# A two-layer decoder step: layer 0's second half by block products in twelve slices, layer 1's weight sums on VectorE

## The chip, the cores and the metric

The kernel runs on one core of a Trainium2 chip. The metric is the device time of one execution in microseconds; lower is better. TensorE (PE) multiplies matrices, VectorE (DVE) and ScalarE (ACT) do elementwise work, GpSimd (POOL) issues some DMAs, and SyncE (SP) issues the rest.

## The reference, cut to what matters

Two layers work on 1024 prompt tokens and on 8 sample tokens with the same weights. Each layer has a mixer and a SwiGLU FFN, with a norm before and after each:

```python
def swiglu(h, w_gu, w_down):
    gate, up = jnp.split(h @ w_gu, 2, axis=-1)
    return (jax.nn.silu(gate) * up) @ w_down
...
        hn = rmsnorm(h, g[0])
        if l < N_A:
            mix, S = a_mixer(...)      # gated linear recurrence, and attention into 256 memory tokens
        else:
            mix = b_mixer(...)         # stick-breaking attention, and attention into 256 memory tokens
        h = h + rmsnorm(mix, g[1])
        h = h + rmsnorm(swiglu(rmsnorm(h, g[2]), w_gu[l], w_down[l]), g[3])
```

The model width is 1024, the inner width of the FFN is 2816. All data is float32.

## The kernel before, in words

**Tokens and tiles.** Activations lie transposed, 128 features to a partition block, so a width of 1024 is a list of eight tiles. The tokens are two groups: group 0 has 512 prompt tokens, group 1 has 512 prompt and the 8 sample tokens (520, handled as two halves of 260). A number is kept as two parts, a rounded one (`fp32r`) and the rest: `split_to` makes both with a ScalarE cast (L227) and a VectorE subtraction (L228). Weights are loaded in blocks of 512x128 and split in the same way (`split_w`, L206 and L207; in `gate_up_w` L501 and L502). Each product is three matmuls: high by high, high by low, low by high.

**The FFN.** The inner width is 22 slices of 128, in five parts: `PARTS = [(0, 5), (5, 5), (10, 4), (14, 4), (18, 4)]`. For each part the slices' gate and up projections are made, then the part's share of the down projection is added to `R`. There are three ways to make a slice:

- `ffn.part` uses `proj` (L220), with two double PSUM banks, and `silu` by Exp, Ln and Exp.
- `gate_up_q` (L464) is the same product in four single banks, with the table's Silu. For a slice of group 1 both take 8 x 2 x 3 x 2 = 96 matmuls of 260 columns. While it runs it steps `sums_w`, the generator that makes the sums of the operands that the next form needs.
- `gate_up_w` (L511) sees gate and up, the two halves of the width and the two halves of the tokens as a 2x2 by 2x2 block product and takes seven products in place of eight: 7 x 4 x 3 = 84 matmuls. It needs four sums of weight blocks and, from `sums_w`, four sums of operand blocks.

`ffn_w` runs a part by the last two forms: its argument `steps` has one entry for each ordinary slice, with how many steps of `sums_w` to take in it, and its argument `first` is the part with which it starts.

**The weights' sums.** `weight_sums(l, parts)` makes the four sums in DRAM: 16 steps for each part of five or four slices, each step one GpSimd DMA, half of them with an addition in the DMA. Before each DMA a one-element copy on GpSimd (L563) ties it to the work of the moment. Layer 0 has them for the parts 2, 3 and 4, layer 1 for all five (80 steps, spread over the middle of the kernel). `gate_up_w` then loads seven blocks for a slice, four of them sums.

**The order of the work.** `weave` interleaves generators in given proportions, in program order. A list scheduler turns that order into a fixed queue for each engine, taking what is ready first by priority of program order; at run time a queue is in order. Around the change the order is: group 0's queries for layer 1 (`b0.heads`) with the end of group 1's output projection (`o1.finish`); group 0's two attentions (`b0.sb`, `b0.mem`), woven with the parts 0 and 1 of group 1's FFN of layer 0; that FFN's parts 2 to 4; group 0's output projection (`o0.mm`) with group 1's norm, its K/V projection and its queries; group 1's attention beside group 0's FFN of layer 1; and last group 1's FFN of layer 1 by `ffn_w(1, 1, ...)`, with three ordinary slices and nineteen by products.

**Buffers that matter.** Raw weight blocks have five tiles (`wraw`) and, in `ffn_w`, others by turns; split blocks five (`wspl`) and by turns some of four (`cpool`). The tag `x0` has eight tiles, which before hold the two attentions' split outputs of group 0 from the attention until `o0.mm`. The middle results of a part are tiles of `mpool`, which has five.

Of the kernel before, what the change touches and what calls it, by code (L numbers as in the profile page):

```python
# [18 lines left out]
P = 128  # L19
# [4 lines left out]
def tile_decoder(  # L24
# [204 lines left out]

    def silu(dst, ps, g):  # L230
# [48 lines left out]
    def sums_w(g, xs, ops, YT, ZT):  # L279
# [5 lines left out]
        for k in range(4):  # L285
# [15 lines left out]
            b11, b12, b21, b22 = full(x0, 0), full(x0, h), full(x1, 0), full(x1, h)  # L301
# [150 lines left out]
    def gate_up_q(g, l, f, xt, side, n_side, first):  # L452
# [4 lines left out]
        for j in range(2):  # L457
# [14 lines left out]
            for a in range(2):  # L472
                d = sg[:, a * h : (a + 1) * h]
                if j == 0:
                    act[0] = nc.scalar.activation(d, pp[a][:, :h], AF.Silu)
                else:
                    nc.vector.tensor_mul(d, d, pp[a][:, :h])
# [4 lines left out]
    def gate_up_w(g, l, f, ops, spl, raws):  # L482
# [5 lines left out]
        src = [  # L488
            (w_gu[l][0:512, gate : gate + P], 0), (sums[l][part][0][:, o : o + P], 4), (sums[l][part][1][:, o : o + P], 5),
            (w_gu[l][512:D, gate : gate + P], 1), (sums[l][part][2][:, o : o + P], 6), (sums[l][part][3][:, o : o + P], 2),  # L490
            (w_gu[l][512:D, up : up + P], 3),
        ]

        def weight(j):
            r = raws()
            nc.sync.dma_start(r, src[j][0].rearrange("(k p) m -> p k m", p=P))
            return r.rearrange("p k m -> p (k m)")

        def split(src):
# [3 lines left out]
            return w  # L503

        def product(ps, j, first=False):
            w = split(weight(j))
            i = src[j][1]
# [16 lines left out]
        nc.scalar.activation(sg[:, :h], pa[:, :h], AF.Silu)  # L524
        product(pb, 4)
        dt = T()
        nc.scalar.copy(dt[:, h:n], pd[:, :h])
        gt = T()
        nc.vector.tensor_add(gt[:, h:n], dt[:, h:n], pb[:, :h])
        product(pc, 5)  # L530
        nc.vector.tensor_sub(gt[:, :h], pc[:, :h], dt[:, h:n])
        product(pb, 6)
        act[0] = nc.scalar.activation(sg[:, h:n], gt[:, :h], AF.Silu)
# [41 lines left out]
    class ffn_w:  # L575


        def __init__(self, g, l, x, steps, first, rows, R=None, own=False):
# [3 lines left out]
            self.half = []  # L582

            def YT():
                if rows:
# [5 lines left out]
            self.sums = sums_w(g, x, self.ops, YT, YT if rows else lambda: A(F32R))  # L591

        def spl(self):
            self.n += 1
            if (self.pi or not self.rows) and not self.own and self.n % 8 in (1, 4, 6):
# [9 lines left out]
        def raws(self):  # L605
            self.r += 1
            if not self.rows and self.r % 2:
# [1029 lines left out]
```

## Time and profile before

| | |
|---|---|
| median of three runs | 2450.1 us (2447.81 to 2451.44) |
| profiled execution | 2446.43 us, span 2444.6 us |
| granted TensorE clock | 0.999 |
| TensorE busy | 2412.0 us |
| VectorE busy | 1639.0 us |
| ScalarE busy | 1251.2 us |
| GpSimd busy | 186.1 us |

The span is the time from the first to the last instruction of the program, and the busy times are unions over the engine's instructions. Matmuls overlap, so a matmul's mean duration is longer than the distance from one to the next. In the views below, a group's row ends with its busy time, the mean duration in ns, the idle time before its instructions and what ended that idle time; a row of windows gives for each engine the busy time in a stretch.

### The profile page before, as it was taken

The page shows a single profiled execution, that of the slowest core. Times are in us where ns is not written, and L with a number is a line of the kernel's source. Part 1 is how long each engine was busy: PE and PEld are TensorE (multiplying, and loading weights), DVE is VectorE, ACT ScalarE, POOL GpSimd, SP SyncE. Part 2 cuts the span into 40 slices and gives each one's busy share as a digit, 9 for nine tenths or more (in the row PEclk, how much of TensorE's full clock was granted, in tenths as well). Part 3 has the DMA queues.
Part 4 walks back from the last instruction along what each step waited for, and adds up shares of the span by engine and source line. Part 5 has one row for each costly group of instructions (what it writes and reads, how often), then busy time and mean ns, then how long its engine had stood idle before and what let it go on. Part 6 is the DMA issues. An engine that isn't in the chain of part 4 may idle for free.

```text
span 2444.6 us, 42106 instructions
## 1 busy us (share of the span) xinstructions
PE 2412.0 (99%) x15839; PEld 2159.3 (88%) x15839; DVE 1639.0 (67%) x2987; ACT 1251.2 (51%) x2441; POOL 186.1 (8%) x315
## 2 busy tenths in 40 slices
PE   8999999999999999999999999999999999999998
PEld 6888888888889988999999989877777888999998
DVE  5867557665897686654756686777788467755565
ACT  5547544344445555554434554555555445654445
POOL 1001101101000000111200102121000100000000
PEclk9999999999999999999999999999999999999999
DMA  5454666577746447677766649655354563464542
GB/s 187 120 166 117 161 191 158 134 192 186 209 132 172 123 156 232 179 179 168 196 166 165 202 139 293 196 151 150 99 163 121 145 192 119 140 193 144 148 145 73
DMA packets 534734, 397.42 MB, mean 163 GB/s; under 512 B 21325, under 2 KB 473018, under 8 KB 534530
## 3 DMA queue, kind: packets, MB, share of 16 engines
q1 hardware_dynamic: 505346, 315.02, 43.3%
q0 software_dynamic: 29184, 79.70, 14.1%
q8 instruction: 125, 2.05, 0.3%
q14 instruction: 79, 0.65, 0.1%
HBM read 364.81 MB, written 101.14 MB: 191 GB/s over the span
## 4 chain that ended last, share of the span: by engine, by line
PE 87%; DVE 6%; DMA 3%; issue 2%; ACT 2%; POOL 0%; SPq 0%; DVEq 0%; ACTq 0%; POOLq 0%
PE mm L220 46%; PE q L511 13%; PE q L648 9%; PE q L464 3%; PE mm L1042 2%; PE s L1188 1%; PE s L906 1%; PE s L1385 1%; PE mm L851 1%; PE mm L824 1%; PE s L875 1%; PE q L680 1%; PE s L1351 1%; DVE ws L207 1%; DMA b<-qd 1%
## 5 line engine op out<-in xcount | busy, mean ns | idle before, releaser
L220 PE MATMUL mm<-x,ws 128*128 128x260 f32 (+1 forms) x6240 | 1115.6, 335 | 3.5 <-DVE r L657 1.7
L220 PEld LDWEIGHTS mm<-x,ws 128*128 128x128 f32 x6240 | 941.0, 188 | 123.9 <-DVE x L228 2.1
L206 ACT CAST ws<-w 128x512 fp32r<-128x512 f32 (+1 forms) x652 | 382.3, 588 | 492.1 <-PE mm L220 336.2
L207 DVE TENSOR_TENSOR ws<-w,ws 128x512 fp32r<-128x512 f32 (+1 forms) x652 | 418.6, 648 | 246.0 <-ACT ws L206 232.0
L220 PE MATMUL mm<-m,ws 128*128 128x512 f32 (+1 forms) x1344 | 281.8, 361 | 0.5 <-DVE r L400 0.4
L220 PEld LDWEIGHTS mm<-m,ws 128*128 128x128 f32 x1344 | 217.8, 188 | 37.2 <-issue 1.0
L648 PE MATMUL q<-m,ws 128*128 128x260 f32 (+1 forms) x1824 | 222.0, 282 | 0.0
L648 PEld LDWEIGHTS q<-m,ws 128*128 128x128 f32 x1824 | 219.0, 188 | 1.3 <-DVE t L534 0.7
L502 DVE TENSOR_TENSOR ws<-w,ws 128x512 fp32r<-128x512 f32 x181 | 124.0, 690 | 89.7 <-ACT ws L501 86.3
L501 ACT CAST ws<-w 128x512 fp32r<-128x512 f32 x181 | 111.8, 621 | 110.8 <-PE q L648 31.9
L511 PE MATMUL q<-x,ws 128*128 128x260 f32 (+1 forms) x1188 | 158.1, 282 | 0.0
L511 PEld LDWEIGHTS q<-x,ws 128*128 128x128 f32 x1188 | 148.7, 188 | 0.0
L511 PE MATMUL q<-y,ws 128*128 128x260 f32 x912 | 119.7, 283 | 0.4 <-ACT q L521 0.4
L511 PEld LDWEIGHTS q<-y,ws 128*128 128x128 f32 x912 | 113.6, 188 | 0.9 <-ACT q L521 0.6
L464 PE MATMUL q<-x,ws 128*128 128x260 f32 (+1 forms) x720 | 91.3, 284 | 0.2 <-DVE r L400 0.2
L464 PEld LDWEIGHTS q<-x,ws 128*128 128x128 f32 x720 | 88.4, 188 | 1.8 <-DVE r L400 0.5
L511 PE MATMUL q<-a,ws 128*128 128x260 f32 (+1 forms) x672 | 87.0, 282 | 0.0
L511 PEld LDWEIGHTS q<-a,ws 128*128 128x128 f32 x672 | 83.2, 188 | 0.0
L657 DVE TENSOR_TENSOR r<-r,q 128x260 f32<-128x260 f32 (+1 forms) x128 | 48.4, 420 | 48.2 <-PE q L648 48.1
L237 DVE TENSOR_SCALAR t<-mm 128x512 f32<-128x512 f32 (+1 forms) x58 | 40.0, 690 | 48.6 <-PE mm L220 48.4
L563 POOL COPY mk<-a 128x1 f32<-128x1 f32 x36 | 21.9, 609 | 640.4 <-ACT a L1241 392.1
L566 POOL DMA_DIRECT2D wsum<-in_w_gu x64 | 58.5, 935 | 114.1 <-DMA wsum<-wsum 89.5
(355 smaller groups left out, 3027.8 us busy)
## 6 DMA issues: line engine op xcount, KB each, us to landing
w<-in_w_gu SPq DMA_DIRECT2D x297, 256.0 KB
w<-in_w_down SPq DMA_DIRECT2D x160, 256.0 KB
wsum<-in_w_gu POOLq DMA_DIRECT2D x72, 512.0 KB, 6.5
w<-wsum SPq DMA_DIRECT2D x104, 256.0 KB
w<-in_w_in_a SPq DMA_DIRECT2D x80, 256.0 KB
w<-in_w_o SPq DMA_DIRECT2D x64, 256.0 KB
wsum<-in_w_gu POOLq DMA_DIRECT2D x24, 640.0 KB, 6.8
wsum<-wsum POOLq DMA_DIRECT2D x24, 512.0 KB, 5.6
```

The source lines that it names most:

```text
L206: nc.scalar.copy(ws[:, 0, :n, :], raw[:, :n, :])
L207: nc.vector.tensor_sub(ws[:, 1, :n, :], raw[:, :n, :], ws[:, 0, :n, :].bitcast(F32))
L220: nc.tensor.matmul(ps[:, a, : PW[g]], wt, xt[k][:, xi, o : o + PW[g]], start=(k == 0 and wi == 0), stop=(k == nk - 1 and wi == 2),)
L237: nc.vector.tensor_scalar(sv(x, g), pv(ps, g), -44.0, None, op0=ALU.max)
L464: ins = nc.tensor.matmul(pp[a][:, :h], wt, xt[k][:, xi, a * h : (a + 1) * h], start=(k == 0 and wi == 0), stop=(k == ND - 1 and wi == 2),)
L501: nc.scalar.copy(w[:, 0, :], src)
L502: nc.vector.tensor_sub(w[:, 1, :], src, w[:, 0, :].bitcast(F32))
L511: nc.tensor.matmul(ps[:, :h], w[:, wj, k * P : (k + 1) * P], x[:, xi, :], start=(first and k == 0 and wi == 0), stop=(k == 3 and wi == 2), ...
L566: nc.gpsimd.dma_start(d, a, accum_op=ALU.add)
L648: nc.tensor.matmul(pp[a][:, :h], wt, mids[k][:, xi, a * h : (a + 1) * h], start=(k == 0 and wi == 0), stop=(k == nf - 1 and wi == 2),)
L657: nc.vector.tensor_add(d, d, pp[a][:, :h])
L1042: nc.tensor.matmul(pb[i][:, a, :], xt[k][:, xi, c * P : (c + 1) * P], ws[:, s, :], start=(k == 0 and wi == 0), stop=(k == ND - 1 and wi == 2),
```

## The change

The operands' sums for group 1's FFN of layer 0 are made beside group 0's attention, in the first three slices of part 0. The parts 0 and 1 are run by `gate_up_q` in place of `ffn.part`, in single banks, with Silu by Exp, Ln and Exp (`lean`) as `ffn.part` had it. The parts 2, 3 and 4 are then run by `gate_up_w` in all their twelve slices; before, three slices of part 2 were ordinary, with the sums made in them.

The sums take the eight tiles of `x0`. The attentions' outputs therefore go to DRAM as they are made (`put`) and come back by `load`, which reads them after part 2 and splits them beside part 4's down projection. The sums read the normalized rows from `o1.R` (`src`) and overwrite them; before, they added the two parts of each operand first.

The 80 steps of `weight_sums(1, ...)` are gone. In layer 1 `gate_up_w` loads the four raw blocks of a slice and makes the sums with four VectorE additions, one into a tile of `npool` and three in place. Where sums are in DRAM (layer 0), the slice is as before. The `lean` form of `gate_up_w` and the tiles in `spare` are for product slices beside an attention; with ten ordinary slices there are none here.

```diff
+    def put(xo, i, cols, src):
+        if isinstance(xo, list):
+            split_to((xo[i][:, 0, cols], xo[i][:, 1, cols]), src)
+            return
+        t = B()[:, : cols.stop - cols.start]
+        nc.scalar.copy(t, src)
+        nc.sync.dma_start(xo[:, i, cols], t)
...
-    def sums_w(g, xs, ops, YT, ZT):
+    def sums_w(g, xs, ops, YT, ZT, src=None):
...
-            b11, b12, b21, b22 = full(x0, 0), full(x0, h), full(x1, 0), full(x1, h)
+            if src:
+                b11, b12, b21, b22 = (src[i][:, c : c + h] for i in (k, k + 4) for c in (0, h))
+            else:
+                b11, b12, b21, b22 = full(x0, 0), full(x0, h), full(x1, 0), full(x1, h)
...
+    def gated(d, x):
+        nc.scalar.activation(d, x, AF.Exp, scale=-1.0)
+        nc.scalar.activation(d, d, AF.Ln, bias=1.0)
+        nc.scalar.activation(d, d, AF.Exp, scale=-1.0)
+        nc.vector.tensor_mul(d, d, x)
...
-                if j == 0:
+                if j == 0 and lean:
+                    if a == 0:
+                        x = T()
+                    nc.vector.tensor_scalar(x[:, a * h : (a + 1) * h], pp[a][:, :h], -44.0, None, op0=ALU.max)
+                    if a:
+                        gated(sg[:, :n], x[:, :n])
+                elif j == 0:
                     act[0] = nc.scalar.activation(d, pp[a][:, :h], AF.Silu)
...
+        ready = sums.get(l, {}).get(part)
...
+        raw = {}
+        if not ready:
+            raw = {"a11": load(block(0, gate)), "a21": load(block(0, up))}
+            raw.update(a22=load(block(512, up)), a12=load(block(512, gate)))
 
         def weight(j):
...
+            if j == 1:
+                s1 = N()[:, :512]
+                nc.vector.tensor_add(s1, raw["a21"], raw["a22"])
+                return s1
+            if j == 2:
+                nc.vector.tensor_add(raw["a21"], raw["a11"], raw["a21"])
+                nc.vector.tensor_add(raw["a11"], raw["a21"], raw["a22"])
+            if j == 5:
+                nc.vector.tensor_add(raw["a11"], raw["a11"], raw["a12"])
+            return raw[("a11", "", "a11", "a12", "a21", "a11", "a22")[j]]
...
+            if self.pi in self.beside and self.r % 9 < 4:
+                return self.spare[self.r % 9 // 2][:, self.r % 9 % 2].rearrange("p (k m) -> p k m", k=4)
+            if (not self.pi or not self.rows) and self.pi not in self.beside and self.r % 2:
                 return B().rearrange("p (k m) -> p k m", k=4)
-            if self.rows and self.pi and self.r % 2:
+            if self.rows and self.r % 2:
...
-            d = xo[H + h]
-            split_to((d[:, 0, :G], d[:, 1, :G]), po)
+            put(xo, H + h, slice(0, G), po)
...
-        def open(self):
-            self.xo = wo_tiles(self.g)
+        def open(self, dram=False):
+            self.xo = tc.dram_tile([P, ND, WID], F32, name=nm("xo")) if dram else wo_tiles(self.g)
+
+        def load(self):
+            d, n, self.xo = self.xo, NG[self.g], []
+            ts = []
+            for k in range(0, ND, 2):
+                t = A()
+                nc.sync.dma_start(t[:, :, :n], d[:, k : k + 2, :n])
+                ts += [t[:, 0, :n], t[:, 1, :n]]
+                yield
+            for t in ts:
+                x = X(self.g)
+                split_to((x[:, 0, :n], x[:, 1, :n]), t)
+                self.xo.append(x)
+                yield
...
-    ws = weight_sums(1, range(5))
...
-    weave((b0.heads(), 8), (o1.finish(), 17), (islice(ws, 4), 4))
-    b0.open()
+    weave((b0.heads(), 8), (o1.finish(), 17))
+    b0.open(True)
+    set_banks(True)
+    fw = ffn_w(1, 0, o1.x, (5, 6, 5, 0, 0, 0, 0, 0, 0, 0), 0, False, beside=(0, 1), src=o1.R)
+    weave((chain(b0.sb(), b0.mem()), 25), (chain(fw.part(0), fw.part(1)), 18))
+    p4 = fw.part(4)
+    back = b0.load()
+    drain(fw.part(2), islice(back, 4))
+    drain(fw.part(3), islice(p4, 4))
+    weave((p4, 4), (back, 8))
     f1 = ffn(1, 0, o1.x)
-    weave((chain(b0.sb(), b0.mem()), 25), (chain(f1.part(0), f1.part(1)), 18), (islice(ws, 34), 35))
-    set_banks(True)
-    fw = ffn_w(1, 0, o1.x, (5, 6, 5), 2, False, f1.R)
-    weave((chain(fw.part(2), fw.part(3), fw.part(4)), 24), (islice(ws, 8), 8))
-    f1.acc = fw.acc
+    f1.R, f1.acc = fw.R, fw.acc
     set_banks(False)
```

The other calls of `weave` lose their share of `ws` and are otherwise as before.

89 lines of the change are left out of this document (53 added, 36 removed).

## The prediction

> **What bounds the kernel now.** I read the page first: the busy shares, the chain that ended last and the DMA queues.
>
> ```profile
> span 2444.6 us, 42106 instructions
> PE 2412.0 (99%) x15839; PEld 2159.3 (88%) x15839; DVE 1639.0 (67%) x2987; ACT 1251.2 (51%) x2441; POOL 186.1 (8%) x315
> q0 software_dynamic: 29184, 79.70, 14.1%
> PE 87%; DVE 6%; DMA 3%; issue 2%; ACT 2%; POOL 0%; SPq 0%; DVEq 0%; ACTq 0%; POOLq 0%
> ```
>
> TensorE is busy for 99% of the span and carries 87% of the chain. So a matmul that is removed shortens the kernel by its own time, and work on other engines costs nothing until it makes TensorE wait. The question is therefore twofold: how many matmuls go, and where VectorE, which gets new work, comes near its own limit. The chain in order of time gives the price of a matmul where the change is made (start, length, what):
>
> ```profile
> 1184.33 24.96 PE mm L220 x209
> 1209.29 5.73 PE s L464 x48
> 1215.02 28.70 PE q L464 x240
> 1243.72 10.06 PE q L511 x84
> 1253.79 23.43 PE q L648 x192
> 1277.22 40.22 PE q L511 x336
> ```
>
> L464 is the ordinary slice (48 and 240 records make three slices of 96), L511 the slice by seven block products (84 each), L648 the down projection. There is no gap between the rows: this stretch runs at TensorE's pace, 40.22/336 = 0.1197 us a matmul, 10.06 us a product slice and 34.43/3 = 11.48 us an ordinary one.
>
> The windows show the other engines in the stretches that the change loads or relieves:
>
> ```profile
> core 0: us, PE busy (x) PEld busy (x) DVE busy (x) ACT busy (x) POOL busy (x), PEclk, DMA share, GB/s
> 990.00:1035.00 45.00, 45.00 (x356) 43.17 (x356) 26.51 (x46) 23.21 (x40) 6.45 (x12) 1.00 0.68 182
> 1026.00:1184.00 158.00, 157.35 (x1198) 148.22 (x1196) 88.00 (x166) 83.10 (x171) 22.78 (x48) 1.00 0.68 165
> 1184.00:1209.00 25.00, 25.00 (x210) 24.98 (x209) 24.78 (x63) 11.39 (x27) 7.86 (x9) 1.00 0.78 193
> 1380.80:1404.00 23.20, 23.20 (x193) 22.90 (x191) 16.05 (x30) 10.81 (x17) 2.16 (x4) 1.00 0.74 215
> 1460.00:1547.00 87.00, 86.28 (x690) 83.62 (x690) 59.17 (x102) 41.66 (x73) 23.17 (x33) 1.00 0.99 272
> 1547.00:1900.00 353.00, 346.00 (x1651) 267.67 (x1650) 272.21 (x424) 185.35 (x359) 26.81 (x26) 1.00 0.47 143
> 2280.70:2303.90 23.20, 23.20 (x195) 23.08 (x194) 13.61 (x28) 7.28 (x12) 0.00 (x0) 1.00 0.43 125
> 2303.90:2344.30 40.40, 40.40 (x338) 40.40 (x338) 25.55 (x46) 23.81 (x49) 0.00 (x0) 1.00 0.57 165
> ```
>
> The first two are the attention of the first token group beside the FFN of the second; 1184 to 1209 is the end of its part 1, where most of the operands' sums are made today; 1380 its last down projection; 1460 the K/V projection and heads, with the DMA engines full; 1547 the second attention; the last two a down projection and four product slices of layer 1. The row of 1184 matters most; the sums' lines run from its start to its end:
>
> ```profile
> 1184.42 0.42 DVE L298 TENSOR_TENSOR b<-x 128x260 f32<-128x260 f32 x1
> 1205.26 0.88 DVE L306 TENSOR_TENSOR b<-b,b 128x260 f32<-128x260 f32 x2
> ```
>
> VectorE is busy for 24.78 of 25 us there and TensorE loses nothing. A full VectorE alone is not yet a stall.
>
> **Part 1, three slices more by products.** Layer 0's second half has 13 ordinary slices and 9 product slices; after it, 10 and 12. Three times 96 - 84 = 12 matmuls go: 36 x 0.1197 = **-4.3 us**. All of them lie on the chain, so this counts in full. The down projections keep their count.
>
> **Part 2, the operands' sums beside the attention.** They need, from these groups:
>
> ```profile
> L306 DVE TENSOR_TENSOR b<-b,b 128x260 f32<-128x260 f32 (+1 forms) x48 | 20.0, 419 | 0.1
> L298 DVE TENSOR_TENSOR b<-x 128x260 f32<-128x260 f32 (+1 forms) x48 | 18.4, 419 | 0.0
> L228 DVE TENSOR_TENSOR m<-t,m 128x512 fp32r<-128x512 f32 (+1 forms) x88 | 60.8, 690 | 9.4 <-ACT m L227 8.7
> ```
>
> Each of the 16 steps is one subtraction and one split, 2 x 0.42 us of VectorE: 13.4 us. (L298, which re-adds the two halves of an operand, 16 x 0.42 us, goes: the sums read the normalized rows that still stand in out_proj's tiles.) The gate's clamp and the product come as two halves of 260 in place of one of 520, about 2 x 0.15 us a slice, 3 us over ten; the eight attention outputs lose their VectorE half of the split, 8 x 0.69 = 5.5 us. So VectorE gains some 11 us in a stretch where it now has 158 - 88 = 70 us free. They are concentrated, though: the 16 steps fall into the first three slices. By the row of 990 that stretch goes from 26.5 to some 41 busy us of 45, 91%. Four tiles that the middle results need are freed only as the steps finish, so a late step holds the next slice's evacuation. The bounds of this: nothing, by the row of 1184 (99% busy, no loss), and by the row of 1547, where VectorE is at 77% beside an attention and TensorE idles 7 of 353 us, 2% of the stage's some 190 us, 3.8 us. I take **+0.7 us**, nearer the first because the ten slices' matmuls do not read the sums at all.
>
> The Silu beside the attention is Exp, Ln, Exp as it is before, so ScalarE gets only 16 casts of 0.41 us. The four single banks replace two double ones, with the same two groups in flight: nothing.
>
> **Part 3, the attention's output through DRAM.** Eight copies and stores replace eight splits; four loads and eight splits come back beside the last down projection. The stores stand on SP's queue before later weight loads and wait for a ScalarE copy; with ten raw and split buffers ahead of TensorE (5 + 5, 24 matmuls or 2.9 us each) a wait of a few us is covered. The eight splits add 8 x 0.69 = 5.5 us to VectorE's 16.05 of 23.2: 21.6, it still fits. If they came late, out_proj would wait, and this seam is already bare:
>
> ```profile
> 1404.03 0.76 DVE L657 TENSOR_TENSOR r<-r,q 128x260 f32<-128x260 f32 x2 [0.73 <-PE q L648]
> 1404.93 5.79 PE L220 MATMUL mm<-x,ws 128*128 128x512 f32 x24 [0.90 <-DVE r L657]
> ```
>
> TensorE waits 0.90 us there for the last evacuation. Bounds: 0, and 5.5 us if all splits came after it. I take **+0.2 us**: the splits need tiles that the products free before that projection begins, so they can go early in it.
>
> **Part 4, layer 1's weight sums.** Eighty GpSimd DMA steps go, with their one-element copies. What this can give is TensorE's idle time in the stretches where they run: 0.65 us in 1026:1184 and 0.72 us in 1460:1547, where DMA is at 0.99. Bounds 0 and -1.4; I take **-0.7 us**. On POOL's own queue only the cache page loads of the second attention stand behind these steps; they can but come earlier. Against this VectorE gets four additions of 128x512 in each of 19 product slices. These are the rows for a slice:
>
> ```profile
> L502 DVE TENSOR_TENSOR ws<-w,ws 128x512 fp32r<-128x512 f32 x181 | 124.0, 690 | 89.7 <-ACT ws L501 86.3 <-DMA w<-wsum 1.0 <-DMA w<-in_w_down 1.0
> L501 ACT CAST ws<-w 128x512 fp32r<-128x512 f32 x181 | 111.8, 621 | 110.8 <-PE q L648 31.9 <-PE q L511 25.8 <-DMA w<-wsum 19.3
> L267 DVE TENSOR_TENSOR st<-st,n 128x512 f32<-128x512 f32 (+1 forms) x91 | 62.1, 690 | 2.1 <-ACT n L266 1.3
> L529 DVE TENSOR_TENSOR t<-t,q 128x260 f32<-128x260 f32 (+1 forms) x33 | 13.8, 419 | 10.8 <-PE q L511 9.5 <-ACT t L527 1.3
> 2234.52 1.29 DVE L502 TENSOR_TENSOR ws<-w,ws 128x512 fp32r<-128x512 f32 x2
> ```
>
> An addition costs 0.69 us (L267, the same form). Counted by durations a slice needs 7 x 0.69 (splits) + 4 x 0.69 (additions) + 4 x 0.42 + 0.69 = 9.96 us, against 10.06 of TensorE. But two in a row take 1.29, not 1.38: the second starts 0.60 after the first. The pair of 1404.03 does the same for 260 elements: 0.76 - 0.42 = 0.34. By starts it is 11 x 0.60 + 4 x 0.34 + 0.60 = 8.6 us, which leaves 1.5 us a slice for waits.
>
> Here a rule weighs against the change. The Trainium skill, "VectorE: DVE Perf Modes", section "The DRAIN you can't avoid", says that the next operation does not start until the pipe is empty, so that what counts is the number of operations. The row of 2234.52 shows an overlap of 0.09 us; by the rule a slice would be at 9.96 us and every wait would reach TensorE. The row decides here, and the third rival below is priced from the durations.
>
> What can wait: the cast of a summed operand (0.62 us, L501) lies between its addition and its split, three times a slice, some 2.4 us if the queue holds nothing in between. But the additions need only raw blocks that are loaded a slice ahead, so they can stand in today's idle time (40.40 - 25.55 us in four slices), as the sums do in the row of 1184. Over a whole part there is room: 25.55 + 13.61 + 11.0 = 50.2 of 63.6 us. Bounds: 0, and the price in the third rival; I take **+0.3 us**, nearest to the full row without a loss. Loads fall from seven to four a slice; nothing is late there.
>
> **The sum.** -4.3 + 0.7 + 0.2 - 0.7 + 0.3 = -3.8, say **-4**. The profiled run took 2446.4 us, 1.8 around its span of 2444.6; changed, 2442.4. It is 3.7 below the median 2450.1 of the runs, so against that median I forecast 2446.
>
> **Rivals.** *All of it is kept:* no new loss, and the waits beside the DMA go as well: -4.3 - 1.4 = -5.7, or 2444.4. For it speaks the row of 1184; against it, that five stretches must all stay covered.
>
> *The attention stage loses it:* steps, attention and slices share VectorE at 91% in 45 us, and what is lost there TensorE cannot make up. By the 2% of 1547 it gives 3.8, by twice that in the fuller stretch 7.6: 2450 to 2454, and with the reload late too, 2457.
>
> *VectorE becomes the bound of layer 1's last stage (slower):* its queue is in order, and the evacuations stand in it behind splits of later products.
>
> ```profile
> 2250.64 0.42 DVE L534 TENSOR_TENSOR t<-t,q 128x260 f32<-128x260 f32 x1
> 2251.71 3.06 PE L511 MATMUL q<-y,ws 128*128 128x260 f32 x24
> 2251.91 0.37 ACT L518 ACTIVATE q<-q 128x260 f32<-128x260 f32 x1 [0.20 <-PE q L511]
> ```
>
> L534 must have read its bank before L518 refills it for the third product, which starts 1.44 us into the row of 2251.71, at 2253.15. That leaves about 1.7 us of delay a part; beyond it TensorE goes at VectorE's pace. It decides from 10.06 us of VectorE a slice. At 9.96 + 1.25 us of uncovered waits it is 17 slices x 1.15 - 4 parts x 1.7 = +12.8, net +8.5 or 2458.6; with all three hand-offs bare (12.4 us) 17 x 2.3 - 6.8 = +32. Against it: the starts, and the idle time into which the additions fit. The first mechanism of the change cannot fail to act: the matmuls are written out.
>
> **How the numbers follow.** 0.2% is 4.9 us, about what a measurement of this kernel tells from no change. My forecast, -4 give or take 3, has 0.46: 0.17 of it below -4.9, 0.27 within, 0.02 above. All kept: 0.20, faster. The attention stage: 0.14, of which 0.04 within and 0.10 slower. VectorE's bound: 0.20, slower. So 0.37 faster, 0.31 the same, 0.32 slower. The range goes from 2440 (all kept, and the 3.7 us of spread between profiled and median runs) to 2462, just past the third rival's moderate price; its full price stays outside.
>
> **What would show it.** In the changed profile four product slices should stand at 40.2 to 40.6 us in layer 1, with VectorE at 34 to 40 of them; the second half of layer 0 should show 336 L511-type matmuls in part 2 too; the first 45 us of the first attention should keep TensorE's idle time under 1 us; the seam to out_proj should stay near 0.9 us; POOL's DMA share should fall by more than half. I am wrong if product slices in layer 1 take over 10.3 us each, or if the first attention ends later by more than 2 us.

## The result and the profile after

Over 12 runs of each kernel the changed one takes 2443.45 us (2442.33 to 2445.95), the one before 2448.4 us (2445.22 to 2454.34). The ratio is 0.998, with a 95% interval of 0.9971 to 0.9989: faster by about 0.2%, which is the size of effect that the prediction called the limit of a measurement. The forecast of 2446 lies 2.5 us above. In the profiled executions, which its sum was made for, the span went from 2444.6 to 2440.6 us: -4.0, as forecast. That exact agreement is partly luck: a second profiled execution of the changed kernel has a span of 2441.9 us, 2.7 below, and two of the stages that make up the -4.0 scatter by as much as they moved.

The page of the changed kernel, the same parts as before:

```profile
span 2440.6 us, 41807 instructions
PE 2408.4 (99%) x15803; PEld 2155.0 (88%) x15803; DVE 1687.5 (69%) x3089; ACT 1264.4 (52%) x2476; POOL 97.4 (4%) x155
q0 software_dynamic: 12544, 33.56, 5.8%
PE 86%; DVE 7%; issue 2%; DMA 2%; ACT 2%; POOL 0%; SPq 0%; DVEq 0%; ACTq 0%; POOLq 0%
```

TensorE has 36 matmuls fewer and is still the chain; VectorE has 48.5 us more; GpSimd's queue takes 5.8% of the DMA engines' time in place of 14.1%. The chain of waits through layer 0's second half (start, length, what):

```profile
1185.83 24.95 PE q L709 x209
1210.78 40.34 PE q L552 x336
1251.12 23.20 PE q L709 x192
1274.32 40.37 PE q L552 x336
1314.70 23.20 PE q L709 x192
1337.90 40.34 PE q L552 x336
```

L552 is the line of the product slices now (L511 before), L709 the down projection. All three parts are four product slices, 336 records, with no gap; each takes 0.12 to 0.15 us more than the 40.22 of before. The windows of the stretches that the prediction used (columns as there):

```profile
core 0: us, PE busy (x) PEld busy (x) DVE busy (x) ACT busy (x) POOL busy (x), PEclk, DMA share, GB/s
991.00:1036.00 45.00, 44.70 (x354) 42.70 (x354) 34.15 (x77) 27.15 (x54) 0.00 (x0) 1.00 0.36 109
1185.80:1210.80 25.00, 25.00 (x212) 25.00 (x211) 13.09 (x30) 9.24 (x18) 0.00 (x0) 1.00 0.89 253
1378.00:1401.20 23.20, 23.18 (x193) 22.96 (x192) 18.41 (x35) 11.89 (x19) 2.29 (x2) 1.00 0.59 188
1457.00:1544.00 87.00, 86.70 (x692) 84.07 (x693) 59.63 (x103) 42.19 (x74) 0.00 (x0) 1.00 0.58 180
2236.80:2277.10 40.30, 40.30 (x338) 40.24 (x337) 32.27 (x58) 24.31 (x50) 0.00 (x0) 1.00 0.43 125
2277.10:2300.30 23.20, 23.20 (x194) 23.07 (x194) 17.95 (x35) 6.64 (x11) 0.00 (x0) 1.00 0.29 82
```

The sums that filled VectorE in the row of 1184 are gone from there (13.09 of 25 us) and now run from 987.2 to 1008 us; the row of 991 (34.15 of 45) has twelve of the sixteen steps. In 1457 the DMA share fell from 0.99 to 0.58. The two last rows hold layer 1's additions: VectorE at 32.27 of 40.30, TensorE full.

For the experiments the span is cut at five points that every trace shows: A, the first matmul of group 0's K/V rows (912.4 us before); P, the end of part 1's down projection; B, the start of the last matmul of layer 0's last down projection; b1, the first score matmul of the second attention; C, the first gate matmul of the last FFN. The table gives the time between them, in us, one profiled execution each; the last column is the five slices of part 1 in the last FFN.

| kernel | A to P | P to B | B to b1 | b1 to C | C to end | part 1 |
|---|---|---|---|---|---|---|
| before | 296.85 | 194.46 | 149.85 | 513.06 | 377.96 | 50.55 |
| changed | 297.79 | 190.54 | 148.47 | 511.60 | 379.22 | 51.78 |
| changed, again | 297.78 | 190.53 | 148.50 | 511.34 | 380.12 | 52.90 |
| layer 1's sums by DMA | 305.86 | 191.56 | 155.27 | 511.68 | 378.12 | 50.40 |
| the same, with a gap | 298.77 | 190.57 | 150.37 | 512.72 | 378.57 | 50.41 |
| the same, moved later | 305.51 | 190.54 | 179.98 | 513.47 | 377.76 | 50.40 |
| layer 1's additions alone | 296.91 | 194.26 | 148.41 | 512.65 | 379.58 | 52.22 |
| three ordinary slices back | 297.81 | 194.71 | 148.49 | 512.13 | 378.75 | 51.38 |
| one addition more | 297.84 | 190.49 | 148.51 | 512.56 | 380.94 | 53.10 |
| four additions more | 297.85 | 190.54 | 148.39 | 513.01 | 379.24 | 51.11 |
| eight additions more | 297.73 | 190.53 | 148.39 | 513.26 | 415.41 | 62.46 |
| sums spread | 297.35 | 190.53 | 148.45 | 510.82 | 379.89 | 52.21 |
| raw blocks in the other pool | 297.79 | 190.54 | 148.45 | 510.42 | 378.97 | 51.17 |
| both of these | 297.32 | 190.55 | 148.42 | 510.98 | 378.48 | 50.65 |

Three columns repeat to 0.1 us where nothing touches them, so a difference of 0.4 us is readable there. The column b1 to C still runs from 510.4 to 513.3 in the ten kernels without layer 1's DMA steps, which edit nothing there: differences of 2 us in it say nothing. Changed against before is +0.94, -3.92, -1.38, -1.46 and +1.26, and +0.55 ahead of A (A itself lies between 912.0 and 914.5): -4.0 in all. The four stages that the prediction's sum speaks of give -3.1 of it; the other -0.9 come from the two stretches that scatter.

### The profile page after: what moved, and what is told of

It is laid out like the page before. It is cut to its first block, busy times and chain, and to the rows that moved or that the text cites. A ratio compares the mean times of both kernels' runs of the same rounds, so it can differ in the third digit from the quotient of the medians.

```text
span 2440.6 us, 41807 instructions
## 1 busy us (share of the span) xinstructions
PE 2408.4 (99%) x15803; PEld 2155.0 (88%) x15803; DVE 1687.5 (69%) x3089; ACT 1264.4 (52%) x2476; POOL 97.4 (4%) x155
## 4 chain that ended last, share of the span: by engine, by line
PE 86%; DVE 7%; issue 2%; DMA 2%; ACT 2%; POOL 0%; SPq 0%; DVEq 0%; ACTq 0%; POOLq 0%
PE mm L220 40%; PE q L552 14%; PE q L709 11%; PE q L481 6%; PE mm L1102 2%; PE s L1248 1%; PE s L967 1%; DVE ws L207 1%; DMA w<-in_w_gu 1%; PE s L1445 1%; PE s L936 1%; PE mm L912 1%; PE mm L885 1%; PE q L741 1%; PE s L1411 1%
## 5 line engine op out<-in xcount | busy, mean ns | idle before, releaser
L220 PE MATMUL mm<-x,ws 128*128 128x512 f32 (+1 forms) x5280 | 989.9, 344 | 4.1 <-DVE r L718 1.6
L220 PEld LDWEIGHTS mm<-x,ws 128*128 128x128 f32 x5280 | 822.5, 188 | 123.4 <-DVE x L228 2.1
L709 PE MATMUL q<-m,ws 128*128 128x260 f32 (+1 forms) x2304 | 284.1, 283 | 0.1
L709 PEld LDWEIGHTS q<-m,ws 128*128 128x128 f32 x2304 | 277.7, 188 | 2.3 <-DVE t L589 0.9
L220 PE MATMUL mm<-m,ws 128*128 128x512 f32 x864 | 219.8, 402 | 0.2 <-DVE r L411 0.2
L552 PE MATMUL q<-y,ws 128*128 128x260 f32 x1488 | 194.7, 283 | 0.9 <-ACT r L716 0.6
L552 PEld LDWEIGHTS q<-y,ws 128*128 128x128 f32 x1488 | 184.9, 188 | 1.4 <-ACT r L716 0.8
L481 PE MATMUL q<-x,ws 128*128 128x260 f32 (+1 forms) x1392 | 182.0, 286 | 0.2 <-DVE r L411 0.2
L481 PEld LDWEIGHTS q<-x,ws 128*128 128x128 f32 x1392 | 172.3, 188 | 2.5 <-DVE r L411 0.5
L552 PE MATMUL q<-x,ws 128*128 128x260 f32 (+1 forms) x1296 | 172.8, 282 | 0.0
L552 PEld LDWEIGHTS q<-x,ws 128*128 128x128 f32 x1296 | 162.4, 188 | 0.0
L718 DVE TENSOR_TENSOR r<-r,q 128x260 f32<-128x260 f32 (+1 forms) x144 | 54.5, 420 | 43.4 <-PE q L709 43.2
L228 DVE TENSOR_TENSOR m<-t,m 128x512 fp32r<-128x512 f32 (+1 forms) x88 | 60.8, 691 | 6.8 <-ACT m L227 6.4
L275 DVE TENSOR_TENSOR st<-st,n 128x512 f32<-128x512 f32 (+1 forms) x91 | 62.2, 691 | 2.1 <-ACT n L274 1.3
```

The costliest lines, as they stand in the source:

```text
L220: nc.tensor.matmul(ps[:, a, : PW[g]], wt, xt[k][:, xi, o : o + PW[g]], start=(k == 0 and wi == 0), stop=(k == nk - 1 and wi == 2),)
L228: nc.vector.tensor_sub(dst[1], src, dst[0].bitcast(F32))
L275: nc.vector.tensor_add(acc[:, :n], acc[:, :n], t[:, :n])
L481: ins = nc.tensor.matmul(pp[a][:, :h], wt, xt[k][:, xi, a * h : (a + 1) * h], start=(k == 0 and wi == 0), stop=(k == ND - 1 and wi == 2),)
L552: nc.tensor.matmul(ps[:, :h], w[:, wj, k * P : (k + 1) * P], x[:, xi, :], start=(first and k == 0 and wi == 0), stop=(k == 3 and wi == 2), ...
L709: nc.tensor.matmul(pp[a][:, :h], wt, mids[k][:, xi, a * h : (a + 1) * h], start=(k == 0 and wi == 0), stop=(k == nf - 1 and wi == 2),)
```

## The experiments

**The changed kernel again**, as the level for the others.

> The changed kernel once more, to see how far a stage's time repeats between two profiles. Theory (stage readings hold to some tenths of a microsecond): span 2440 to 2442, ratio to the kernel before 0.998; from the start of the product slices of layer 0's second half to the first output projection 191.6 us, from there to the last stage 665.7, and the last stage's parts 0 and 1 some 1.5 us longer than in the kernel before. Rival (they are noise): these three differ from the first profile by a microsecond or more, in any direction.

Measured: 0.9983 (0.9974 to 0.9992), 2445.3 us. The table shows where two executions of one kernel differ: 0.9 us after C, in part 1's slices above all. The three stages from A to b1 repeat to 0.03 us.

**Three ordinary slices back.**

```diff
-    fw = ffn_w(1, 0, o1.x, (5, 6, 5, 0, 0, 0, 0, 0, 0, 0), 0, False, beside=(0, 1), src=o1.R)
+    fw = ffn_w(1, 0, o1.x, (5, 6, 5, 0, 0, 0, 0, 0, 0, 0, 0, 0, 0), 0, False, beside=(0, 1), src=o1.R)
```

> The changed kernel with the three first slices of part 2 of layer 0's second half ordinary again (13 ordinary, 9 by products); everything else stays, the operands' sums beside the attention too. Theory A: 36 matmuls more at 0.1197 us, +4.3 us, ratio 0.9998, all of it between the start of part 2 and its down projection. Rival D (the gain came from somewhere else, such as the part 2 that lost its sums' steps): less than 2 us of it comes back, ratio under 0.9988.

Measured: 0.9991 (0.9981 to 1.0), 2447.36 us; P to B goes from 190.54 to 194.71, +4.17. Its chain:

```profile
1210.41 34.43 PE q L481 x288
1244.84 10.09 PE q L552 x84
```

Three ordinary slices take 34.43 us and a product slice 10.09; the saving of three is 34.43 - 3 x 10.09 = 4.16. The matmuls are worth what they were priced at, within 0.15 us, and the stages beside this one don't move.

**Layer 1's additions alone**: before, with the weight sums made by VectorE in layer 1 and nothing else of the change.

```diff
-            (w_gu[l][0:512, gate : gate + P], 0), (sums[l][part][0][:, o : o + P], 4), ...
+            raw = {"a11": load(block(0, gate)), "a21": load(block(0, up))}
+            raw.update(a22=load(block(512, up)), a12=load(block(512, gate)))
...
+                nc.vector.tensor_add(s1, raw["a21"], raw["a22"])
...
-    ws = weight_sums(1, range(5))
```

> The kernel before with one part of the change alone: layer 1's weight sums by VectorE, no sums of layer 1 by DMA; layer 0's second half keeps its nine product slices. Theory A: -2.8 + 1.7 = -1.1 us against the kernel before, ratio 0.9995. Rival C (VectorE bounds the last stage): product slices of layer 1 over 10.3 us each, and a ratio of 1.002 or more. Rival B: ratio 1.0007, the loss of the last stage alone.

Measured: 0.999 (0.9981 to 0.9999), 2446.46 us. From A to P nothing comes back (296.91 against 296.85 us); the stage from B to b1 gets back 1.44 us, and the last FFN loses 1.62. The median is 2.5 us lower, but the stages of the profile add up to -0.3: how much this part alone gains is not settled. VectorE as the bound of that FFN is out: its parts of four slices take 40.46 to 40.61 us.

**Layer 1's weight sums by DMA in the changed kernel**: everything else of the change stays, the 80 steps come back where they were (the other calls of `weave` get their share of `ws` back too).

```diff
+    ws = weight_sums(1, range(5))
...
-    weave((chain(b0.sb(), b0.mem()), 25), (chain(fw.part(0), fw.part(1)), 18))
+    weave((chain(b0.sb(), b0.mem()), 25), (chain(fw.part(0), fw.part(1)), 18), (islice(ws, 34), 35))
...
-    drain(fw.part(2), islice(back, 4))
-    drain(fw.part(3), islice(p4, 4))
+    weave((chain(fw.part(2), islice(back, 4), fw.part(3), islice(p4, 4)), 24), (islice(ws, 8), 8))
```

> The changed kernel, but layer 1's weight sums made by GpSimd DMAs as before, in the same places. Theory A (the two traces, stage by stage): without these DMAs the stretch from the first output projection to the last stage was 2.8 us shorter, and the last stage was some 1.7 us longer because the four raw blocks of a slice come late; so putting the DMAs back costs +2.8 - 1.7 = +1.1 us against the changed kernel, ratio 0.9985, the middle stretch back to 668.4 us and the last stage back to the time of the kernel before. Rival B (the DMAs touch nothing; the middle stretch moved because the queues were ordered anew): the middle stretch stays at 665.7, and the kernel becomes 1.7 us faster than the changed one, ratio 0.9973.

Measured: 1.0028 (1.0016 to 1.004), 2456.39 us. Both theories missed by over 10 us. The loss lies in two stages: A to P, 8.1 us more than changed, and B to b1, 6.8 more. The timelines of TensorE, VectorE and ScalarE at the first place (start, length, instruction, and in brackets the idle time before it and what ended it):

```profile
1210.23 0.62 ACT L546 CAST ws<-w 128x512 fp32r<-128x512 f32 x1 [5.79 <-DMA w<-in_w_gu]
1210.88 1.51 DVE L547 TENSOR_TENSOR ws<-w,ws 128x512 fp32r<-128x512 f32 x2 [5.71 <-ACT ws L546]
1212.30 0.76 DVE L718 TENSOR_TENSOR r<-r,q 128x260 f32<-128x260 f32 x2
1212.87 5.62 PE L709 MATMUL q<-m,ws 128*128 128x260 f32 x30 [5.92 <-DVE r L718]
```

A raw block of the next part lands late; its cast and split wait. Behind that split in VectorE's queue stands the evacuation L718, whose bank the current down projection needs: TensorE waits 5.92 us for an evacuation whose own data had long been there. Then 30 matmuls take 5.62 us, 0.187 each in place of 0.1197, and the windows show why:

```profile
core 0: us, PE busy (x) PEld busy (x) DVE busy (x) ACT busy (x) POOL busy (x), PEclk, DMA share, GB/s
1185.00:1215.00 30.00, 24.08 (x191) 23.86 (x190) 12.00 (x28) 8.35 (x18) 4.66 (x10) 0.92 1.02 263
1212.80:1218.40 5.60, 5.53 (x31) 5.56 (x32) 3.54 (x8) 1.73 (x4) 1.44 (x3) 0.65 0.90 267
1218.40:1224.00 5.60, 5.60 (x48) 5.60 (x48) 3.52 (x7) 3.25 (x8) 0.88 (x1) 1.00 0.92 276
```

After the wait the granted clock is 0.65 for 5.6 us and then full again: the slow restart costs 30 x (0.187 - 0.1197) = 2.0 us more. 5.9 + 2.0 is nearly all of the stage's 8.1. From B to b1 the trace has one other long wait, and a slow stretch behind it (the row of the wait, then the window after it):

```profile
1510.14 0.27 PE L1389 MATMUL s<-ident,ks 128*8 128x128 f32 x1 [2.87 <-DVE ks L1372]
1510.10:1516.00 5.90, 5.86 (x20) 4.67 (x21) 3.53 (x7) 0.62 (x1) 0.00 (x0) 0.71 1.07 371
```

A wait of 2.87 us is followed by 5.9 us at a clock of 0.71, 1.7 us more. In all TensorE idles 7.14 us in that stage, in place of 2.33 in the changed kernel; the idle time and the clock are 6.5 of the 6.8 us.

The Trainium skill, "TensorE: Matmul & The Clock Gate", Part 1, says that an idle array falls to half rate and needs about 3.4 us of work to come back; 0.65 over 5.6 us would be half rate for 3.9 us and 0.71 over 5.9 us for 3.4, so the trace agrees.

**The same, with eight steps moved later**, to find out whether the transfers beside the load do it.

```diff
-    weave((chain(fw.part(2), islice(back, 4), fw.part(3), islice(p4, 4)), 24), (islice(ws, 8), 8))
+    drain(fw.part(2), islice(back, 4))
+    drain(fw.part(3), islice(p4, 4))
...
-    weave((kv_proj(1, xk1), 8), (islice(ws, 10), 11))
+    weave((kv_proj(1, xk1), 8), (islice(ws, 18), 18))
```

> The changed kernel with layer 1's weight sums made by GpSimd's DMAs again, as in the run with DMA sums, but with none of them in the stretch from the last of part 1's slices to the end of part 3; those eight steps go into the K/V projection instead. Theory A (the 5.9 us wait at the end of part 1's down projection there came of the sums' transfers beside a late weight load, a burst at one place): the wait goes to under 1 us, this stage is 5 us shorter than in that run, and the K/V projection's stage, where the DMA engines are full, gets longer by 0 to 3 us; 2451 to 2454 us, ratio 1.0005 to 1.002. Rival B (the loads of layer 0's product slices are late without any sum beside them, by the order of the loads alone): the wait stays at 5 us or more, 2456 us, ratio 1.003.

Measured: 1.0117 (1.0102 to 1.0133), 2481.31 us. The wait at the end of part 1 stayed (5.0 us), but that decides nothing: the last steps of the 34 beside the attention still ran there, with 9 GpSimd instructions between 1185 and 1215. What it did show is the other end: 18 steps in place of 10 beside the K/V projection cost 25 us in the stage from B to b1 (179.98 against 155.27), which has 26 of the steps in place of 18, since the queries there have eight.

```profile
1460.00:1550.00 90.00, 70.80 (x515) 66.67 (x516) 37.19 (x65) 23.82 (x42) 19.14 (x40) 0.92 0.89 235
```

TensorE idles 19 of 90 us there while the DMA engines are at 0.89, and the clock is 0.92.

**The same, with a gap**: the steps beside the attention end earlier, and parts 2 and 3 take 16.

```diff
-    weave((chain(b0.sb(), b0.mem()), 25), (chain(fw.part(0), fw.part(1)), 18), (islice(ws, 34), 35))
+    weave((chain(b0.sb(), b0.mem()), 25), (chain(fw.part(0), fw.part(1)), 18), (islice(ws, 26), 35))
...
-    weave((chain(fw.part(2), islice(back, 4), fw.part(3), islice(p4, 4)), 24), (islice(ws, 8), 8))
+    p2 = fw.part(2)
+    drain(islice(p2, 3))
+    weave((chain(p2, islice(back, 4), fw.part(3), islice(p4, 4)), 21), (islice(ws, 16), 16))
```

> The changed kernel with layer 1's weight sums made by GpSimd's DMAs, as in the run with DMA sums, but with a gap: 26 of the 34 steps beside the attention, spread so that they end some 40 us before part 1's slices do, and 16 in place of 8 beside parts 2 and 3, the first of them after three slices of part 2. The stretch from 1185 to 1215 us thus holds none of GpSimd's transfers, which the last attempt did not reach. Theory A (the wait of 5 to 6 us at the end of part 1's down projection needs the sums' transfers beside the weight loads): the wait goes to under 1 us, and the ratio from 1.003 to 1.000 (1.002 if parts 2 and 3 lose 2 us to their 16 steps). Rival B (the loads there are late by their own order): the wait stays above 4 us, ratio 1.003.

Measured: 0.9978 (0.9968 to 0.9988), 2444.79 us: better than theory A asked. The same window, and that of the kernel before:

```profile
1185.00:1215.00 30.00, 30.00 (x250) 29.90 (x250) 16.94 (x36) 11.68 (x23) 0.00 (x0) 1.00 0.86 237
1185.00:1215.00 30.00, 30.00 (x254) 30.00 (x253) 27.11 (x67) 12.77 (x30) 8.64 (x11) 1.00 0.85 210
```

No GpSimd transfer, DMA at 0.86 in place of 1.02, TensorE full. The kernel before has the steps there and loses nothing either: its next slices are ordinary, with four blocks each to load in place of seven. So neither the steps nor the product slices' loads make the wait alone; both together do. The placing of 8 steps in 80 goes with 11.6 us, of which 7.1 lie in this stage. Another 4.9 lie from B to b1 (150.37), where the 18 steps are the same: the wait of 2.87 us is 0.3 there. The steps' number doesn't decide that wait; what does, no run isolates.

**One addition more, and four more, in each product slice of layer 1**, repeats of one that is there. They ask where VectorE becomes the bound.

```diff
-                nc.vector.tensor_add(s1, raw["a21"], raw["a22"])
+                for _ in range(5):
+                    nc.vector.tensor_add(s1, raw["a21"], raw["a22"])
```

(With one more, `range(2)`.)

> The changed kernel with one addition of 128x512 more in each product slice of layer 1 (the first sum is made twice). Theory by starts (0.60 us each; four slices show VectorE busy for 32 of 40.3 us): 34.5 of 40.3 us, nothing to see, at most +0.5 us. Rival by durations (0.69 us each, the next starts when the pipe is empty; a slice at 9.96 of 10.06 us already): 10.65 us a slice, 17 x 0.6 - 6.8 = +3.4 us or more.

> The changed kernel with four additions of 128x512 more in each product slice of layer 1 (the first sum is made five times). Theory by starts: 8.6 + 2.4 = 11.0 us of VectorE a slice against 10.06 of TensorE, so VectorE becomes the bound there: 17 x 0.95 less what the down projections win back, +5 to +12 us, with slices of 10.4 to 11 us. Rival by durations: 12.7 us a slice, +30 us or more.

Measured: 0.9988 (0.9979 to 0.9997), 2445.17 us, and 0.9978 (0.9969 to 0.9987), 2443.74 us. Four more cost nothing that can be measured: the last FFN takes 379.24 us, and 380.94 with one more, so that the scatter is larger than any cost. By the 0.60 us from start to start a slice then asks for 8.6 + 4 x 0.6 = 11.0 us of VectorE in 10.06 us of TensorE. The windows of four slices and the down projection behind them:

```profile
2238.40:2278.70 40.30, 40.15 (x335) 39.89 (x334) 39.04 (x73) 23.38 (x51) 0.00 (x0) 1.00 0.42 123
2278.70:2301.90 23.20, 23.20 (x194) 23.07 (x194) 21.52 (x43) 6.63 (x12) 0.00 (x0) 1.00 0.30 85
```

VectorE's work fills the down projection as well (21.52 of 23.20 us), since additions and splits of the next part are pulled into it. The room is that of the whole part. Its timeline shows the distance from start to start:

```profile
2252.55 3.70 DVE L535 TENSOR_TENSOR n<-w,w 128x512 f32<-128x512 f32 x6
```

Six additions in a row take 3.70 us: (3.70 - 0.69) / 5 = 0.60.

**Eight additions more** (`range(9)`), past the room of a part.

> The changed kernel with eight further additions (repeats of one that is there) in each of layer 1's product slices: twelve in all, 13.4 us of VectorE a slice by starts of 0.60. Theory A (VectorE's room is that of a whole part, 63.5 us of four slices and a down projection): 4 x 13.4 + 13.6 = 67.2, so each full part gets about 3.6 us longer, the last stage some 11 to 15 us, ratio to before about 1.003; the stretch of four slices stands at about 44 us or the down projection at 25 or more, with VectorE at 97% or more of both. Rival B (VectorE's room is that of one slice, 10.06 us): each slice takes 13.4 us, four of them 53 us, the last stage some 50 us longer, ratio 1.018. Rival C (additions cost 0.69 us each, because nothing starts before the pipe is empty): 4 x 15.5 + 13.6 = 75.6 us a part, 12 us longer each, the last stage some 45 us longer.

Measured: 1.0113 (1.0097 to 1.0128), 2479.09 us; the last FFN takes 36 us longer, which none of the three theories had. Two parts of it:

```profile
2253.10:2306.00 52.90, 45.72 (x340) 43.68 (x339) 49.50 (x89) 26.40 (x55) 0.00 (x0) 0.94 0.33 94
2306.00:2329.00 23.00, 23.00 (x193) 22.87 (x192) 22.48 (x44) 5.92 (x10) 0.00 (x0) 1.00 0.21 61
2329.00:2371.90 42.90, 41.68 (x340) 40.79 (x339) 41.74 (x77) 23.55 (x50) 0.00 (x0) 1.00 0.36 103
2371.90:2394.70 22.80, 22.80 (x193) 22.80 (x192) 20.39 (x41) 5.93 (x10) 0.00 (x0) 1.00 0.30 85
```

TensorE idles (52.90 - 45.72) + (42.90 - 41.68) = 8.4 us, 4.2 a part, near theory A's 3.6. But its busy time also grew, from 2 x 40.4 to 87.4, with as many matmuls; 5.3 of these 6.6 us are in the first row, where the clock was 0.94: over 52.9 us that is 3.2 us. Theory A had left that out. It doesn't explain the whole: the first two parts lost 16 us, where 7 were expected. The bound lies between 11.0 and 13.4 us of VectorE a slice. Beyond it the waits cost more than their own length.

**The sums spread**: two steps a slice over eight slices in place of 5, 6 and 5 over three. The sums then can't overwrite the rows of `o1.R`, so they add the operand's parts again.

```diff
-    fw = ffn_w(1, 0, o1.x, (5, 6, 5, 0, 0, 0, 0, 0, 0, 0), 0, False, beside=(0, 1), src=o1.R)
+    fw = ffn_w(1, 0, o1.x, (2, 2, 2, 2, 2, 2, 2, 2, 0, 0), 0, False, beside=(0, 1))
```

> The changed kernel with the operands' sums spread over eight slices beside the attention (two steps each) in place of three, made from the split operands as before, since the normalized rows would hold the tiles of the middle results: 16 x 0.42 us more of VectorE in all, but half the load in the first slices. Theory A (the attention stage's loss of 1.1 us comes from VectorE's load in its first 45 us): the stretch from the K/V rows to the start of the product slices goes from 297.8 back to under 297.2 us, ratio 0.9977. Rival E (it comes from the four single banks or the copies to DRAM): still 297.8.

Measured: 0.9979 (0.997 to 0.9988), 2443.24 us; A to P 0.44 us less. About half of the stage's loss comes back, the rest does not.

**Every second raw block of the last FFN in the other pool.** In the changed kernel those of its parts after the first come from `apool` two at a time, and the first of them wait there.

```diff
-            if (not self.pi or not self.rows) and self.pi not in self.beside and self.r % 2:
+            if self.pi not in self.beside and self.r % 2:
```

> The changed kernel, but every second raw block of the last stage goes into the seven tiles of bpool in all parts, not into halves of apool tiles from part 1 on. Theory A (the last stage loses its time where part 1 begins: the first loads into apool wait until the output projection's rows have been transposed for the last time, and the loads behind them on SP's queue wait too, so VectorE's additions and the first products start late): the last stage from its first matmul to the end goes from 379.2 to 380.1 us back to some 378, and the kernel gains 1.2 to 2 us over the changed one, ratio 0.9975. Rival C (the additions fill VectorE): no change, ratio 0.998.

Measured: 0.9976 (0.9966 to 0.9985), 2442.52 us; part 1 takes 51.17 us. From C to the end it is 378.97 us, 0.3 to 1.2 less than in the two profiles of the changed kernel. Theory A asked for some 378; by the times alone this could be scatter. TensorE's waits, in the account of layer 1's additions below, decide it.

**Both of these.**

> The changed kernel with two edits: every second raw block of the last stage in the other pool, and the sums' steps spread evenly, two a slice, over eight slices. Theory A (the two small losses, late loads at the start of the last stage and the first slices of the attention, are apart from each other): part 1's slices of the last stage at about 51.2 us, attention stage at 297.4; ratio 0.997, or 2441 to 2442 us. Rival B (what the single edits showed is scatter): 0.998, 2443 us, with the same two stages as in the changed kernel.

Measured: 0.9952 (0.9938 to 0.9965), 2440.31 us (2438.94 to 2441.05), the lowest median here. The kernel before stood at 2451.43 us beside it, 3 above its median elsewhere, so some 3 of the 7 us between this ratio and 0.998 are the comparison's; against the changed kernel's 2443.45 and 2445.3 it is 3 to 5 us ahead. Set against medians of other comparisons, that lead is not sharp: in profiled spans the kernel with the other pool alone is 0.9 us shorter (2438.4 against 2439.3). Both stages behave as theory A said: 297.32 and 50.65 us. VectorE's additions for part 1, changed and then this kernel:

```profile
2145.50 0.69 DVE L534 TENSOR_TENSOR n<-w,w 128x512 f32<-128x512 f32 x1 [3.82 <-DMA w<-in_w_gu]
2150.55 0.69 DVE L534 TENSOR_TENSOR n<-w,w 128x512 f32<-128x512 f32 x1 [2.95 <-DMA w<-in_w_gu]
```

```profile
2143.22 0.69 DVE L534 TENSOR_TENSOR n<-w,b 128x512 f32<-128x512 f32 x1 [1.72 <-DMA w<-in_w_gu]
2148.17 0.69 DVE L534 TENSOR_TENSOR n<-w,b 128x512 f32<-128x512 f32 x1 [1.08 <-DMA w<-in_w_gu]
```

The first two slices' additions wait for raw blocks, and come some 2 us sooner with the other pool.

## Why the prediction was right, point by point

The products carry the result, and they are priced right. Of the small terms the last two are mis-sized, by 0.7 us down and 1.0 up; they nearly cancel, and that the total came out at -4.0 is luck to that extent.

**The products** (-4.3): right. P to B gave -3.92, the undoing +4.17.

**The operands' sums beside the attention** (+0.7): +0.94 us. The size is right. The prediction expected VectorE at 41 of 45 us; the load is shorter and denser than that. The stretch that holds all sixteen steps, in the kernel before, the changed one and the one with the sums spread:

```profile
986.00:1009.00 23.00, 23.00 (x171) 21.69 (x170) 12.84 (x24) 11.30 (x20) 3.59 (x5) 1.00 0.72 201
986.00:1009.00 23.00, 22.70 (x163) 21.06 (x162) 22.88 (x57) 16.14 (x36) 0.00 (x0) 1.00 0.50 151
986.00:1009.00 23.00, 23.00 (x161) 21.30 (x160) 18.36 (x40) 12.92 (x25) 0.00 (x0) 1.00 0.56 164
```

VectorE is busy for 22.88 of 23 us, TensorE loses 0.30 us, and with the steps spread it loses nothing there. So the forecast that it idles under 1 us in the first 45 held, and the reason, VectorE's load, holds for this part. The other half of the loss stays when the sums are spread: TensorE idles 0.65 us from A to P before, 1.31 changed and 1.05 spread. What the other half is, no run shows.

**The output through DRAM** (+0.2): not contradicted, but too small to be seen alone. P to B is 194.71 us with thirteen ordinary slices and 194.26 with layer 1's additions alone, which has no reload: 0.45 us for the reload and all else that differs there. The seam to the output projection:

```profile
1401.52 0.76 DVE L718 TENSOR_TENSOR r<-r,q 128x260 f32<-128x260 f32 x2 [0.64 <-PE q L709]
1402.43 4.86 PE L220 MATMUL mm<-x,ws 128*128 128x512 f32 x20 [0.82 <-DVE r L718]
```

0.82 us in place of 0.90, and VectorE at 18.41 of 23.20 in the last down projection. The splits hide.

**The relief of the DMA engines** (-0.7): mis-sized by half, and not where the bound was taken from. B to b1 is 148.4 to 148.5 us in ten kernels without the steps and 149.85 before: -1.4. The bound of -1.4 was the idle time of two stretches. The first, 1026:1184 with 0.65 us, gave nothing: with layer 1's additions alone TensorE idles 0.65 us from A to P, as before. The second stage gave twice the 0.72 us that the prediction read from 1460:1547. Two waits of the kernel before that are gone without the steps:

```profile
1467.44 0.66 PE L1315 MATMUL s<-ident,t 128*128 128x128 f32 x4 [0.43 <-ACT t L1310]
1553.60 1.14 PE L1351 MATMUL s<-a,a 128*128 128x128 f32 x4 [0.70 <-DMA a<-ksc]
```

The second is a load for the second attention, 6.6 us behind the end of the window that was read. That the size met the far end of the bound is chance. The further -1.46 between b1 and C is within that stage's scatter and was luck.

**Layer 1's additions** (+0.3): mis-sized, and the step that failed is "nothing is late there". The last FFN lost 1.26 us, and up to 2.98 in the kernels that add no more than one operation to it. The prediction looked at VectorE and found room, rightly: over four slices and a down projection it forecast 50.2 us of VectorE, and the two last rows of the changed kernel's windows have 32.27 + 17.95 = 50.2. More of it lies in the down projection than it thought, so the slices alone stand at 32.27 rather than 34 to 40; they take 40.3 to 40.5 us, as forecast. The loss lies in part 1's five slices: 51.1 to 53.1 us, 52.1 in the mean of seven kernels, against 50.4 to 50.6 in the four with the sums by DMA. The changed kernel's trace shows how a late load gets there:

```profile
2153.41 0.62 ACT L546 CAST ws<-w 128x512 fp32r<-128x512 f32 x1 [3.28 <-DVE w L538]
2157.57 0.64 ACT L716 COPY r<-q 128x260 f32<-128x260 f32 x2
2158.26 3.12 PE L552 MATMUL q<-y,ws 128*128 128x260 f32 x24 [0.62 <-ACT r L716]
```

With sums from DRAM each product needs one block; now the second needs two more at once. VectorE's addition of 2150.55 waits for them, ScalarE's cast waits 3.28 us for the additions, and behind the casts in ScalarE's queue stands an evacuation of part 0's down projection (L716), for which TensorE waits 0.62 us. All seven kernels have this last wait, of 0.07 to 1.68 us; the four with sums by DMA don't, nor do the two with the raw blocks in the other pool. In the five of the seven that change nothing in layer 1's slices it is the cast's wait less 2.64 to 2.66 us: 0.62 of 3.28, in the repeat 1.55 of 4.20, with additions alone 0.85 of 3.50, with three ordinary slices 0.10 of 2.74, with the sums spread 1.07 of 3.72. In the other pool the cast waits 1.49, and TensorE not at all. So the late loads are the cause of this wait and of its scatter. Some 0.5 us of the slices' loss is no wait and stays open: without their idle time they take 50.9 to 51.1 us.

**The rivals.** "All of it is kept" was right about the waits beside the DMA (1.4 us) and wrong that no new loss comes. "The attention stage loses it" asked for 3.8 us or more; the stage lost 0.9. "VectorE becomes the bound" did not happen, and its point of decision, 10.06 us a slice, was wrong: a part of four slices and a down projection shares its room, and 11.0 us a slice still cost nothing.

The rule of the Trainium skill that was weighed, in "VectorE: DVE Perf Modes", "The DRAIN you can't avoid", would have put four additions more at 9.96 + 2.76 = 12.7 us a slice, an estimate with each operation for its full 0.69; the measured distance of 0.60 decided rightly. The same section adds that a next operation that is not held back starts earlier. The prediction did not weigh that; the starts 0.60 us apart agree with it.

**What the sum did not have**: that the two halves of the change depend on each other. Part 4 alone gained 2.5 us in the median (0.999); the rest with the DMA steps as they had stood lost 7.4 (1.0028), and with eight of the steps moved gained 4.0 (0.9978). The whole gained 3.7 and 5.0. So removing the steps was worth 11 us or next to nothing, by where they would have stood.

## What to carry to other kernels

Price an engine's room over the stretch in which its work can be moved, not over one slice: queues that run ahead even out a slice that is too full. When loads or background transfers are regrouped, look for the place where a cast or split that waits for a load stands ahead of an evacuation in one queue, because there a transfer off the path stops TensorE: both large losses here, 5.92 us on VectorE's queue and up to 1.68 on ScalarE's, came that way. Divide the span at points that every trace shows and learn each stage's scatter before a difference of 1 us is given a cause.

## What the runs showed of the hardware

The price of a wait is not its length alone: 5.92 us of waiting were followed by 5.6 us at a granted clock of 0.65, so that it cost about 7.9, and 2.87 us by 5.9 us at 0.71, about 4.6. The wait of 1.55 us in the repeat's last FFN left the clock at 1.00. With eight additions more, 7.2 us of idle time in one stretch went with 5.3 us more of busy time, of which the clock explains 3.2.

And the price of a background transfer is not proportional: the 18 steps from B to b1 cost 1.4 us in the kernel before, 1.9 in the one with a gap and 6.8 in the one with all the steps back where they were; eight further ones cost 25 us, about 3 us each.
